# State-space input matrices of a two-layer encoder: factor rows reread from DRAM in place of turns on TensorE

## The chip, the cores and the metric

One core of a Trainium2 chip. The metric is device time of one execution in microseconds, lower is better. TensorE (PE) multiplies and turns tiles, VectorE (DVE) and ScalarE (ACT) work on elements, GpSimd (POOL) hardly takes part, and SyncE (SP) issues every transfer of this kernel to 16 DMA engines.

## The reference, cut to what matters

Two layers of a gated encoder on 256 positions of 1024 channels. Each layer has a joint input projection, three branches (retention, latent attention, and the state-space branch "S5"), gates, an output projection and a SwiGLU FFN. The changed part is the input side of S5: 64 groups of 16 channels each drive a 64-dimensional complex state, forward and backward.

```python
    bb_re = coef_re[..., None] * b_re - coef_im[..., None] * b_im      # per group (64 states, 16 channels)
    bb_im = coef_re[..., None] * b_im + coef_im[..., None] * b_re
    bu_re = jnp.einsum('bsgc,gpc->bsgp', u_g, bb_re)
    bu_im = jnp.einsum('bsgc,gpc->bsgp', u_g, bb_im)
...
    _, _, xr, xi = lax.associative_scan(combine, (a_re_t, a_im_t, bu_re, bu_im), reverse=reverse, axis=1)
    return jnp.einsum('bsgp,gcp->bsgc', xr, c_re) - jnp.einsum('bsgp,gcp->bsgc', xi, c_im)
```

The kernel cuts the 256 positions into 32 chunks of 8. What a chunk adds to the state at its end is one product of the chunk's inputs, (position s, channel c) = 128 rows, with a matrix whose entry is the complex power a^(7-s) times bb[c]. These matrices, one of 128 x 256 numbers per group, are the "input matrices": 16 tiles per layer, of four groups each (index qq), [128, 1024] in SBUF.

## The kernel before

The main stream is a chain of weight products. A weight tile of 512 KB is loaded into one of five buffers `raw` (L121, the helper that every transfer goes through; all are issued by SyncE in one order), ScalarE casts it to a rounded part `wh` (L663), VectorE takes the rest `wl` (L664), and TensorE makes three passes (L668 to L670), 24 products a tile. Tiles `s` of 128 x 1024 come from a pool of 17.

The S5 branch is a generator that is advanced in the background: after each weight tile it gets credit in proportion to the tile's time and issues steps until that is used up. So its instructions lie between the main products, on every engine. Its turns and small products use a pool of two PSUM banks (p5). Its steps in a layer:

- `s5_params`: powers a^1 to a^8 and the coefficients, 128 partitions = (direction, group).
- `s5_tables`: turns the powers by TensorE so that (direction, state) is on the partitions, loads B in that order (four loads of 256 KB in pieces of 64 bytes), makes bb (`BB`; L338 to L340), stores it (`bbd`), and sums and differences for a product of complex numbers in three multiplications.
- `s5_wt`, for each qq: three products on VectorE (L518, L521), a sum (L526), eight turns by TensorE (L531) into two banks, two copies by ScalarE (L533).
- In layer 0 the branch's input u is turned (L420, L429), and each input matrix is made just before its four products (L447); the result is copied (L454), turned, and copied to the scan's layout (L463). In layer 1 the tables do not depend on u, so they are made during layer 0's FFN and the start of layer 1, stored to DRAM (`wtd`) and reread.
- `s5_out`: output kernels; `kd` is one of its tables, stored and reread as `wt<-kd` with a pattern of 8 blocks x 16 rows: `ap=[[16, 8], [480, 16], [240, 2], [1, 128]]`. `t_bb` rereads bb.

Of the kernel before, what the change touches and what calls it, by code (L numbers as in the profile page):

```python
# [12 lines left out]
ALU = mybir.AluOpType  # L13
# [4 lines left out]
P = 128  # L18
# [60 lines left out]
class Kern:  # L79
# [108 lines left out]
    def table(self, k):  # L188
        """A table of rope or rel, loaded for a layer."""
# [21 lines left out]
    def s5_params(self, l):  # L211
        """Natural layout [(dir, g), p]: discretised A, its powers, and the input coefficient."""
        nc, V = self.nc, self.nc.vector
        N = SP_
        nt = lambda k: self.s(N, "nt_" + k)
# [38 lines left out]
        cf = self.s(2 * SP_, "nt_cf").rearrange("p (r q) -> p r q", r=2)  # L254
# [17 lines left out]
    def load_b(self, l, *bs):  # L272
        """The loads of the input matrices, as calls."""
        f = lambda t, k, d: self.dma(t[d * 64:d * 64 + 64].rearrange("p (g c) -> p g c", c=GC),
                                     self.a[k][l, d].rearrange("g p c -> p g c"))
        return [lambda t=t, k=k, d=d: f(t, k, d) for t, k in zip(bs, ("s5_b_re", "s5_b_im")) for d in range(2)]

    def load(self):
        if self.loads:
            f = self.loads.pop(0)  # L280
            if f:
                f()

    def s5_tables(self, l):
        """Tables of a layer.  Group index gamma = (qh, q, g4) for the natural g = (qh, g4, q);
        position index s' = 7 - s inside a chunk of 8."""
        nc, V, A = self.nc, self.nc.vector, self.nc.scalar
        pn, cf = yield from self.s5_params(l)
        yield 4.0
        PX = self.s4().rearrange("p (j d g) -> p j d g", j=8, d=2)  # L290
        for b in range(2):
            ps = self.bank(self.p5)
            for j in range(4):
                nc.tensor.matmul(ps[:, j * P:(j + 1) * P], pn[:, b * 4 + j].rearrange("p r q -> p (r q)"),
                                 self.perm, start=True, stop=True)
            A.copy(PX[:, b * 4:b * 4 + 4].rearrange("p j d g -> p (j d g)"), ps)
        CF = self.s(2 * 64, "t_cf").rearrange("p (r g) -> p r g", r=2)
        ps = self.bank(self.p5)
        nc.tensor.matmul(ps[:, 0:P], cf.rearrange("p r q -> p (r q)"), self.perm, start=True, stop=True)
        for r in range(2):  # L300
            for d in range(2):
                A.copy(CF[d * 64:d * 64 + 64, r, :], ps[r * 64:r * 64 + 64, d * 64:d * 64 + 64])
        PW = self.s4().rearrange("p (r s g) -> p r s g", r=2, s=8)
        A8 = self.s(2 * 64, "t_a8").rearrange("p (r g) -> p r g", r=2)
        A8s = self.s(2 * 64, "t_a8s").rearrange("p (r g) -> p r g", r=2)
        for r in range(2):
            nc.gpsimd.memset(PW[0:64, r, 0, :], 1.0 - r)
            nc.gpsimd.memset(PW[64:128, r, 7, :], 1.0 - r)
            rows = slice(r * 64, r * 64 + 64)
            A.copy(PW[0:64, r, 1:8, :], PX[rows, 0:7, 0, :])  # L310
            A.copy(PW[64:128, r, 6::-1, :], PX[rows, 0:7, 1, :])
        for d in range(2):
            rows = slice(d * 64, d * 64 + 64)
            A.copy(A8[rows, 0, :], PX[0:64, 7, d, :])
            A.copy(A8[rows, 1, :], PX[0:64, 7, d, :])
            A.mul(A8s[rows, 0, :], PX[64:128, 7, d, :], -1.0)
            A.copy(A8s[rows, 1, :], PX[64:128, 7, d, :])
        PXD = self.t(self.dr, [P, 1024], "pxd", 2)
        self.dma(PXD, PX.rearrange("p j d g -> p (j d g)"))
        if l == 0 and self.nl >= 0:  # L320
            while "b" not in self.cx:
                yield None
            br, bi = self.cx.pop("b")
        else:
            br, bi = self.s4(), self.s4()
            for f in self.load_b(l, br, bi):
                f()
        BB = [self.s4(), self.s4()]
        for qh in range(2):
            c = slice(qh * 512, qh * 512 + 512)  # L330
            nat = lambda t: t[:, c].rearrange("p (h q c) -> p h q c", h=4, q=8)
            natt = lambda t: t.rearrange("p (h q c) -> p h q c", h=4, q=8)
            cfv = lambda r: (CF[:, r, qh * 32:qh * 32 + 32].rearrange("p (q h) -> p h q", h=4)
                             .unsqueeze(3).to_broadcast([P, 4, 8, GC]))
            for r, (x, y, op) in enumerate(((br, bi, ALU.subtract), (bi, br, ALU.add))):
                yield 1.9
                t1, t2 = self.s(512, "tm"), self.s(512, "tm")
                V.tensor_tensor(natt(t1), cfv(0), nat(x), ALU.mult)  # L338
                V.tensor_tensor(natt(t2), cfv(1), nat(y), ALU.mult)
                V.tensor_tensor(BB[r][:, c].rearrange("p (q h c) -> p h q c", q=8, h=4), natt(t1), natt(t2), op)  # L340
        BBD = self.t(self.dr, [P, 2048], "bbd", 2)
        for r in range(2):
            self.dma(BBD[:, r * 1024:(r + 1) * 1024], BB[r])
        PD = self.s(512, "t_pd").rearrange("p (s g) -> p s g", s=8)
        V.tensor_tensor(PD, PW[:, 1], PW[:, 0], ALU.subtract)
        V.scalar_tensor_tensor(PW[:, 1], PW[:, 1], -1.0, PW[:, 0], ALU.mult, ALU.subtract)
        BS = self.s4()
        V.tensor_tensor(BS, BB[0], BB[1], ALU.add)
        return dict(PW=[PW[:, 0], PW[:, 1], PD], PXD=PXD, A8=A8, A8s=A8s, BB=[BS, BB[1], BB[0]], BBD=BBD)

    def s5_out_tables(self, l, tb, qh):
        """Per half: BB2 [(ri,p), d, gamma, c], C1 = [c_re; c_im], C2 = [c_im; c_re] (d, gamma, co), and the
        power tables AL = [a^j_re; -a^j_re], BE = [-a^j_im; -a^j_im] with j ascending for d = 0, descending for d = 1."""
        nc, V, A = self.nc, self.nc.vector, self.nc.scalar
        BB2 = self.s(2 * 528, "t_bb2", 1).rearrange("p (d x) -> p d x", d=2)
        for d in range(2):
            for r in range(2):
                self.dma(BB2[r * 64:r * 64 + 64, d, 0:512],
                                  tb["BBD"][d * 64:d * 64 + 64, r * 1024 + qh * 512:r * 1024 + qh * 512 + 512])
            nc.gpsimd.memset(BB2[:, d, 512:528], 0.0)  # L360
# [1118 lines left out]
```

## Time and profile before

| | |
|---|---|
| median of 3 runs | 1432.98 us (1431.25 to 1438.25) |
| span of the profiled execution | 1436.6 us |
| TensorE, VectorE, ScalarE busy | 94%, 72%, 56% |
| DMA | 260.86 MB, mean 182 GB/s |

The span is that of one profiled execution. Busy times of TensorE are modelled and can overlap, so the start times in a timeline tell more than the sum of the durations. A share of DMA is the mean over the core's 16 engines.

### The profile page before, as it was taken

How to read it: one execution, taken by the hardware profiler on the slowest of the kernel's cores; microseconds unless marked ns; L12 is line 12 of the kernel's file. 1: busy time of each engine (PE TensorE's matmuls, PEld its weight loads, DVE VectorE, ACT ScalarE, POOL GpSimd, SP SyncE). 2: the span in 40 equal slices, each digit the busy share in tenths (PEclk: the TensorE clock that was granted, in tenths of full speed). 3: DMA queues.
4: the chain of work that ended last, by engine and by line, in shares of the span. 5: the costliest groups of instructions: out<-in, count | busy, mean ns of one | idle time of the engine just before them, and what ended most of it. 6: DMA issues, size and time to landing. Idle time of an engine off the chain costs nothing. (4 is left out here: it accounts for less than half of the span.)

```text
span 1436.6 us, 27883 instructions
## 1 busy us (share of the span) xinstructions
PE 1355.2 (94%) x11250; PEld 1255.3 (87%) x11250; DVE 1032.8 (72%) x1891; ACT 806.9 (56%) x1339; POOL 4.4 (0%) x33
## 2 busy tenths in 40 slices
PE   8899998888999999999999989789999999999997
PEld 7866778877888999999999867778988899999997
DVE  6877867877688579978668547878777556677644
ACT  3666566874664465545446677796583344444432
POOL 0000000000000000000000000000000000000000
PEclk9999998999999999999999999999999999999999
DMA  7954232646776699766678884376687567566652
GB/s 197 239 162 123 72 103 88 173 140 168 204 213 189 205 215 255 209 195 198 184 218 268 248 264 121 99 189 180 168 234 202 172 197 212 161 182 188 181 171 75
DMA packets 433892, 260.86 MB, mean 182 GB/s; under 512 B 61714, under 2 KB 413284, under 8 KB 433764
## 3 DMA queue, kind: packets, MB, share of 16 engines
q1 hardware_dynamic: 433764, 259.09, 64.3%
q8 instruction: 88, 1.44, 0.4%
q14 instruction: 40, 0.33, 0.1%
HBM read 231.53 MB, written 27.53 MB: 180 GB/s over the span
## 5 line engine op out<-in xcount | busy, mean ns | idle before, releaser
L668 PE MATMUL pw<-s,wh 128*128 128x256 f32 x2472 | 716.5, 291 | 16.2 <-ACT wh L663 11.6
L670 PE MATMUL pw<-s,wl 128*128 128x256 f32 x2472 | 703.6, 286 | 5.3 <-DVE wl L664 5.2
L669 PE MATMUL pw<-s,wh 128*128 128x256 f32 x2472 | 703.6, 285 | 0.0
L663 ACT CAST wh<-raw 128x1024 fp32r<-128x1024 f32 (+4 forms) x394 | 380.5, 972 | 464.9 <-PE pw L669 292.4
L664 DVE TENSOR_TENSOR wl<-raw,wh 128x1024 fp32r<-128x1024 f32 (+4 forms) x394 | 443.1, 1128 | 229.7 <-ACT wh L663 225.8
L668 PEld LDWEIGHTS pw<-s,wh 128*128 128x128 f32 x2472 | 472.6, 191 | 33.4 <-ACT wh L663 13.8
L670 PEld LDWEIGHTS pw<-s,wl 128*128 128x128 f32 x2472 | 472.7, 192 | 11.6 <-DVE wl L664 7.0
L669 PEld LDWEIGHTS pw<-s,wh 128*128 128x128 f32 x2472 | 473.1, 192 | 6.4 <-issue 4.9
L708 PE MATMUL pw<-s,wh 128*128 128x256 f32 x256 | 71.9, 281 | 0.0
L709 PE MATMUL pw<-s,wh 128*128 128x256 f32 x256 | 71.9, 281 | 0.0
L710 PE MATMUL pw<-s,wl 128*128 128x256 f32 x256 | 71.9, 281 | 0.0
L564 DVE TENSOR_TENSOR wy<-s,s 128x512 f32<-128x512 f32 x64 | 42.4, 687 | 13.6 <-PE pa L624 9.6
L709 PEld LDWEIGHTS pw<-s,wh 128*128 128x128 f32 x256 | 48.2, 188 | 0.0
L710 PEld LDWEIGHTS pw<-s,wl 128*128 128x128 f32 x256 | 48.2, 188 | 0.0
L708 PEld LDWEIGHTS pw<-s,wh 128*128 128x128 f32 x256 | 48.2, 188 | 0.0
L531 PE MATMUL p<-ident,wy 128*128 128x128 f32 x256 | 36.8, 276 | 11.9 <-ACT s L463 11.6
L531 PEld LDWEIGHTS p<-ident,wy 128*128 128x128 f32 x256 | 28.8, 141 | 17.0 <-ACT s L463 13.7
L492 ACT COPY s<-s 64x256 f32<-64x256 f32 (+1 forms) x64 | 40.7, 636 | 4.7 <-DVE s L478 3.8
L565 DVE TENSOR_TENSOR tm<-s,s 128x512 f32<-128x512 f32 x64 | 43.1, 687 | 0.0
L566 DVE TENSOR_TENSOR wy<-wy,tm 128x512 f32<-128x512 f32 x64 | 42.7, 685 | 0.0
L743 ACT ACTIVATE s<-ev 128x512 fp32r<-128x512 f32 x46 | 29.1, 633 | 19.5 <-DVE ev L1326 12.5
L668 PE MATMUL pw<-wh,s 128*128 128x512 f32 (+1 forms) x96 | 35.6, 373 | 4.5 <-ACT s L1074 4.5
(282 smaller groups left out, 1586.8 us busy)
## 6 DMA issues: line engine op xcount, KB each, us to landing
raw<-in_w_in SPq DMA_DIRECT2D x122, 512.0 KB
raw<-in_ffn_w_gu SPq DMA_DIRECT2D x88, 512.0 KB
raw<-in_w_branch SPq DMA_DIRECT2D x48, 512.0 KB
raw<-in_s_w_glu SPq DMA_DIRECT2D x32, 512.0 KB
raw<-in_ffn_w_down SPq DMA_DIRECT2D x32, 512.0 KB
wt<-kd SPq DMA_DIRECT2D x64, 128.0 KB
raw<-in_w_out SPq DMA_DIRECT2D x16, 512.0 KB
wtd<-wt SPq DMA_DIRECT2D x16, 512.0 KB
```

What stands on the lines that cost most here:

```text
L531: T.transpose(ps[:, i * P:(i + 1) * P], W[i % 2][:, gp * 2 + i // 2].rearrange("p s c -> p (s c)"), self.ident)
L564: V.tensor_tensor(y[:, :, js, :], tv(0), cv(C1), ALU.mult)
L565: V.tensor_tensor(t2, tv(1), cv(C2), ALU.mult)
L566: V.tensor_tensor(y[:, :, js, :], y[:, :, js, :], t2, ALU.add)
L663: self.nc.scalar.copy(hi, src)
L664: self.nc.vector.tensor_tensor(lo, src, hi.bitcast(F32), ALU.subtract)
L668: T.matmul(ps, lh, rh, start=first, stop=False)
L669: T.matmul(ps, lh, rl, start=False, stop=False)
L670: T.matmul(ps, ll, rh, start=False, stop=last)
L708: T.matmul(o, wh[:, k, c], xh, start=(half == 0 and m == 0 and k == 0), stop=(k == 3), **f)
L709: T.matmul(o, wh[:, k, c], xl, start=False, stop=(k == 3), **f)
L710: T.matmul(o, wl[:, k, c], xh, start=False, stop=(k == 3), **f)
```

## The change

The input matrices are made directly with (position, channel) on the partitions. The powers are stored to DRAM as `pwd`, 8 rows (positions) of 16384, and bb as `bbd`, 16 rows (channels) of 16384, each row ordered by qq, direction, group, (re, im), state. For each qq two loads of 512 KB bring them back, one repeating each power row over 16 partitions, the other repeating the 16 channel rows 8 times; VectorE then makes two products of 1024 columns and a difference and a sum of 512. No turn and no PSUM copy is left in `s5_wt`. The rows are written by 16 transfers for the powers and 2 x 16 for bb in each layer, each of 8 x 8 pieces of 512 bytes. B is loaded in its natural order, (direction, group) on the partitions, at the head of the S5 branch, in two loads of 512 KB; bb for the output side, which needs (re/im, state) on the partitions, is now made by 16 turns and 16 copies per layer and stored as `bb2d` (two transfers). The columns of the input matrices are ordered (direction, group, re/im...), so the copy L454 permutes. The scratch tiles of `s5_params` share one tile `s`.

```diff
     def s5_tables(self, l):
+        br, bi = self.s4(), self.s4()
+        for t, k in ((br, "s5_b_re"), (bi, "s5_b_im")):
+            self.dma(t, self.a[k][l].rearrange("d g p c -> (d g) (p c)"), pin=l > 0)
         pn, cf = yield from self.s5_params(l)
+        PN = self.s4().rearrange("p (s x) -> p s x", s=8)
...
+        flat = pn.rearrange("p j r q -> p j (r q)")
+        A.copy(PN[0:64, 1:8, :], flat[0:64, 0:7, :])
+        A.copy(PN[64:128, 6::-1, :], flat[64:128, 0:7, :])
+        def rows(t, r0, src):
+            t = t[:, :]
+            for i in range(16):
+                at = r0 * 16384 + i // 4 % 2 * 8192 + i // 8 * 512 + i % 4 * 128
+                self.dma(bass.AP(tensor=t.tensor, offset=t.offset + at, ap=[[1024, 8], [16384, 8], [1, 128]]),
+                         src[i * 8:i * 8 + 8])
+        PWD = self.t(self.dr, [8, 16384], "pwd", 2)
+        rows(PWD, 0, PN)
...
+            rows(BBD, hf * 8, B.rearrange("p c r q -> p c (r q)"))
...
+        for c4 in range(4):
+            ps = self.bank(self.p5)
+            for i in range(4):
+                c = c4 * 4 + i
+                T.transpose(ps[:, i * P:(i + 1) * P], BB[c // 8][:, c % 8].rearrange("p r q -> p (r q)"), self.ident)
...
+                    A.copy(half[qh][:, d, :, :, c4 * 4:c4 * 4 + 4].rearrange("p q h c -> p c h q"), v[:, :, d, qh])
+            yield 1.0
+        for qh in range(2):
+            self.dma(BB2D[:, qh * 1024:(qh + 1) * 1024], half[qh].rearrange("p d q h c -> p (d q h c)"))
...
     def s5_wt(self, tb, qq):
-        k1 = self.s(512, "tm")
-        V.tensor_tensor(k1.rearrange("p (g s c) -> p g s c", g=4, s=8), pwv(0), bbv(0), ALU.mult)
-        for r in range(2):
-            V.tensor_tensor(w, pwv(1 + r), bbv(1 + r), ALU.mult)
-        V.tensor_tensor(w, w, k1.rearrange("p (o x) -> p o x", o=1).to_broadcast([P, 2, 512]), ALU.add)
...
+        for k, ap in (("PWD", [[16384, 8], [0, 16], [1, 1024]]), ("BBD", [[0, 8], [16384, 16], [1, 1024]])):
+            t = self.s4()
+            src = tb[k][:, :]
+            self.dma(t, bass.AP(tensor=src.tensor, offset=src.offset + qq * 1024, ap=ap))
...
+        V.tensor_tensor(k1, bb, by(0), ALU.mult)
+        V.tensor_tensor(k2, bb[:, :, ::-1, :], by(1), ALU.mult)
         wt = self.s(1024, "wt")
-        for gp in range(2):
-            ps = self.bank(self.p5)
-            for i in range(4):
-                T.transpose(ps[:, i * P:(i + 1) * P],
-                            W[i % 2][:, gp * 2 + i // 2].rearrange("p s c -> p (s c)"), self.ident)
-            A.copy(wt[:, gp * 512:(gp + 1) * 512], ps)
+        V.tensor_tensor(w[:, :, 0, :], k1[:, :, 0, :], k2[:, :, 0, :], ALU.subtract)
+        V.tensor_tensor(w[:, :, 1, :], k1[:, :, 1, :], k2[:, :, 1, :], ALU.add)
```

What moves in the order of the queue, at two places. First SyncE near the start of the program, around the first S5 tables of layer 0. A tile's name has a running number, so the same weight tile has another number in the two kernels: raw_603 of before is raw_662 after. Before:

```order
L121 DMA raw_520<-in_w_in 128x8x128
L121 DMA s_71_353<-in_rope 128x1024
L121 DMA raw_603<-in_w_in 128x8x128
L121 DMA s_88_424<-in_s_b_re 64x64x16
L121 DMA pxd_422<-s_79_383 128x1024
L121 DMA s_88_424<-in_s_b_re 64x64x16
L121 DMA s_89_425<-in_s_b_im 64x64x16 x2
L121 DMA dud_357<-s_75_358 128x1024
L121 DMA raw_685<-in_w_in 128x8x128
L121 DMA raw_747<-in_w_in 128x8x128
```

After, at the same place:

```order
L121 DMA pwd_321<-s_54_314 8x8x128 x16
L121 DMA s_64_370<-in_rope 128x1024
L121 DMA raw_561<-in_w_in 128x8x128
L121 DMA pxd_423<-s_72_400 128x1024
L121 DMA dud_374<-s_68_375 128x1024
L121 DMA bbd_425<-s_79_426 8x8x128 x16
L121 DMA bbd_425<-s_87_469 8x8x128 x16
L121 DMA dud_374<-s_80_431 128x1024
L121 DMA lg_108_616<-in_ret_decay 128x16
L121 DMA raw_662<-in_w_in 128x8x128
L121 DMA bb2d_540<-s_98_541 128x1024
L121 DMA bb2d_540<-s_99_542 128x1024
```

The weight tile raw_662 stands behind 48 row stores, 32 of which stand behind raw_561, and the next one behind the two stores of turned coefficients. The B loads have gone to the head of the program.

Second, SyncE at the start of layer 1, where input matrices are made ahead (the first rows are the last tiles of one projection's weights; `s<-pwd` and `s<-bbd` are the factor loads, `wtd` the stores of finished matrices). Before:

```order
L121 DMA raw_9209<-in_w_in 128x8x128
L121 DMA raw_9239<-in_w_in 128x8x128
L121 DMA dud_8874<-s_1478_8875 128x1024
L121 DMA raw_9277<-in_w_in 128x8x128
L121 DMA raw_9328<-in_w_in 128x8x128
L121 DMA wtd_9080<-wt_9067 128x1024
L121 DMA raw_9365<-in_w_in 128x8x128
```

After:

```order
L121 DMA raw_9110<-in_w_in 128x8x128
L121 DMA dud_8769<-s_1458_8770 128x1024
L121 DMA s_1484_8948<-pwd_5525 128x1x1024
L121 DMA wtd_8846<-wt_8843 128x1024
L121 DMA s_1485_8950<-bbd_5830 128x1x1024
L121 DMA s_1502_9060<-pwd_5525 128x1x1024
L121 DMA dud_8769<-s_1472_8852 128x1024
L121 DMA s_1503_9062<-bbd_5830 128x1x1024
L121 DMA raw_9148<-in_w_in 128x8x128
L121 DMA s_1522_9178<-pwd_5525 128x1x1024
L121 DMA wtd_8959<-wt_8956 128x1024
L121 DMA s_1523_9180<-bbd_5830 128x1x1024
```

Four factor loads now stand between two weight tiles, and two more before the next. Of the 32 factor loads of layer 1's matrices 18 stand among layer 0's FFN weights and 14 behind the first weights of layer 1.

## Rows read from the trace of the kernel before

**Rows 1.** The page: engines' busy time, and the group of the turns (us, mean ns, wait).

```profile
PE 1355.2 (94%) x11250; PEld 1255.3 (87%) x11250; DVE 1032.8 (72%) x1891; ACT 806.9 (56%) x1339; POOL 4.4 (0%) x33
...
L531 PE MATMUL p<-ident,wy 128*128 128x128 f32 x256 | 36.8, 276 | 11.9 <-ACT s L463 11.6
```

**Rows 2.** Table of windows: busy us per engine, granted clock, DMA share.

```profile
36.00:252.00 216.00, 196.14 (x1336) 164.38 (x1336) 164.64 (x346) 134.60 (x252) 0.54 (x4) 0.96 0.49 131
...
550.00:750.00 200.00, 199.96 (x1691) 199.66 (x1690) 156.21 (x204) 95.61 (x119) 0.00 (x0) 1.00 0.71 205
750.00:830.00 80.00, 79.76 (x570) 72.92 (x569) 55.82 (x85) 49.05 (x79) 0.65 (x4) 1.00 0.83 251
...
36.00:72.00 36.00, 31.94 (x212) 29.44 (x213) 31.13 (x66) 22.11 (x46) 0.00 (x0) 0.91 1.04 239
```

**Rows 3.** Waits of TensorE, 36 to 252 us: total, times, longest.

```profile
PE p L531 <- ACT s L463: 11.6, 7, 1.8
PE pw L668 <- ACT wh L663: 6.2, 2, 3.9
```

**Rows 4.** Timeline of TensorE in layer 0's FFN: start, duration.

```profile
648.86 0.28 PE L670 MATMUL pw<-s,wl 128*128 128x256 f32 x1
648.98 1.03 PE L531 MATMUL p<-ident,wy 128*128 128x128 f32 x8
649.77 0.36 PE L668 MATMUL pw<-s,wh 128*128 128x256 f32 x1
649.97 0.28 PE L669 MATMUL pw<-s,wh 128*128 128x256 f32 x1
```

**Rows 5.** Windows of the turns at L531 alone.

```profile
36.00:252.00 216.00, 19.86 (x128) 14.24 (x128) 0.96 0.49 131
540.00:828.00 288.00, 16.93 (x128) 14.53 (x128) 1.00 0.76 220
```

**Rows 6.** Groups by shape: busy us, mean ns.

```profile
L526 DVE TENSOR_TENSOR wy<-wy,tm 128x1024 f32<-128x1024 f32 x32 | 39.1, 1221 | 0.3
...
L518 DVE TENSOR_TENSOR tm<-s,s 128x512 f32<-128x512 f32 x32 | 21.7, 685 | 0.1
...
L533 ACT COPY wt<-p 128x512 f32<-128x512 f32 x64 | 35.8, 587 | 1.2 <-PE p L531 0.5
```

**Rows 7.** Timeline of SyncE's issues at the start: start, duration.

```profile
34.33 0.38 SPq L121 DMA_DIRECT2D raw<-in_w_in  x1
34.75 0.73 SPq L121 DMA_DIRECT2D s<-in_s_b_re  x1
...
39.96 6.16 SPq L121 DMA_DIRECT2D s<-in_s_b_im  x2
...
49.21 7.47 SPq L121 DMA_DIRECT2D raw<-in_w_in  x5
58.21 0.34 SPq L121 DMA_DIRECT2D bbd<-s  x1
```

**Rows 8.** Waits of ScalarE, 36 to 62 us: total, times, longest.

```profile
ACT wh L663 <- DMA raw<-in_w_in: 10.6, 2, 10.1
```

**Rows 9.** Table of windows around the first hole, columns as in rows 2.

```profile
52.00:56.00 4.00, 2.05 (x18) 1.85 (x16) 3.97 (x8) 0.80 (x1) 0.00 (x0) 1.00 1.04 274
56.00:60.00 4.00, 3.05 (x13) 2.75 (x14) 4.00 (x7) 3.98 (x8) 0.00 (x0) 0.56 1.21 290
```

**Rows 10.** SyncE's issues by transfer: least, median, most ns.

```profile
L121 SPq DMA_DIRECT2D wt<-kd x64: 569/582/1370, 318.4 to 1127.3; - x64
```

**Rows 11.** Timeline of VectorE: the last step of the powers in layer 0.

```profile
29.31 0.42 DVE L253 TENSOR_TENSOR s<-tm,tm 128x256 f32<-128x256 f32 x1
```

**Rows 12.** DMA, 331 to 339 us, 40 slices of 0.2 us: kd<-ev, then wt<-kd.

```profile
DMA  0000199910000001004004555555823798999999
GB/s 0 0 0 0 67 403 374 365 60 0 0 0 0 0 0 41 0 0 46 0 8 138 177 172 172 177 172 177 110 72 79 161 215 223 279 282 225 215 210 197
```

More of the change, by code (lines that the diff above doesn't have):

```diff
@@ L270, in s5_params @@
         return pn, cf
[L272 to L282, printed above, removed]
     def s5_tables(self, l):
-        nc, V, A = self.nc, self.nc.vector, self.nc.scalar
+        nc, V, A, T = self.nc, self.nc.vector, self.nc.scalar, self.nc.tensor
+        br, bi = self.s4(), self.s4()
+        for t, k in ((br, "s5_b_re"), (bi, "s5_b_im")):
+            self.dma(t, self.a[k][l].rearrange("d g p c -> (d g) (p c)"), pin=l > 0)
         pn, cf = yield from self.s5_params(l)
+        PN = self.s4().rearrange("p (s x) -> p s x", s=8)
+        for d, s0 in ((0, 0), (1, 7)):
+            for r in range(2):
+                nc.gpsimd.memset(PN[d * 64:d * 64 + 64, s0, r * 64:r * 64 + 64], 1.0 - r)
+        flat = pn.rearrange("p j r q -> p j (r q)")
[9 more added lines that the diff above has]
+        rows(PWD, 0, PN)
         yield 4.0
@@ L312, in s5_tables @@
-        for d in range(2):
[L313 to L317, printed above, removed]
+        for d in range(2):
+            rows_ = slice(d * 64, d * 64 + 64)
+            A.copy(A8[rows_, 0, :], PX[0:64, 7, d, :])
+            A.copy(A8[rows_, 1, :], PX[0:64, 7, d, :])
+            A.mul(A8s[rows_, 0, :], PX[64:128, 7, d, :], -1.0)
+            A.copy(A8s[rows_, 1, :], PX[64:128, 7, d, :])
@@ L318, in s5_tables @@
         PXD = self.t(self.dr, [P, 1024], "pxd", 2)
         self.dma(PXD, PX.rearrange("p j d g -> p (j d g)"))
[L320 to L334, printed above, removed]
+        BBD = self.t(self.dr, [16, 16384], "bbd", 2)
@@ L339, in s5_tables @@
[L339 to L346, printed above, removed]
@@ L347, in s5_tables @@
-        BS = self.s4()
-        V.tensor_tensor(BS, BB[0], BB[1], ALU.add)
-        return dict(PW=[PW[:, 0], PW[:, 1], PD], PXD=PXD, A8=A8, A8s=A8s, BB=[BS, BB[1], BB[0]], BBD=BBD)
+                t1, t2 = (self.s(512, "tm").rearrange("p (c q) -> p c q", c=8) for _ in range(2))
+                V.tensor_tensor(t1, cfv(0), nat(x, hf), ALU.mult)
+                V.tensor_tensor(t2, cfv(1), nat(y, hf), ALU.mult)
+                V.tensor_tensor(B[:, :, r, :], t1, t2, op)
+            rows(BBD, hf * 8, B.rearrange("p c r q -> p c (r q)"))
@@ new lines, in s5_tables @@
+            BB.append(B)
+        del br, bi
+        BB2D = self.t(self.dr, [P, 2048], "bb2d", 2)
+        half = [self.s4().rearrange("p (d q h c) -> p d q h c", d=2, q=8, h=4) for _ in range(2)]
+        for c4 in range(4):
[3 more added lines that the diff above has]
+                T.transpose(ps[:, i * P:(i + 1) * P], BB[c // 8][:, c % 8].rearrange("p r q -> p (r q)"), self.ident)
+            v = ps.rearrange("p (c d k h q) -> p c d k h q", c=4, d=2, k=2, h=4)
+            for qh in range(2):
+                for d in range(2):
+                    A.copy(half[qh][:, d, :, :, c4 * 4:c4 * 4 + 4].rearrange("p q h c -> p c h q"), v[:, :, d, qh])
+            yield 1.0
@@ L351, in s5_out_tables @@
+        for qh in range(2):
+            self.dma(BB2D[:, qh * 1024:(qh + 1) * 1024], half[qh].rearrange("p d q h c -> p (d q h c)"))
+        return dict(PWD=PWD, BBD=BBD, BB2D=BB2D, PXD=PXD, A8=A8, A8s=A8s)
     def s5_out_tables(self, l, tb, qh):
@@ L721, in fm_pair_native @@
             self.flush()
-            self.load()
             self.tick(3.5)
@@ L1178, in layer @@
         native = lambda c: self.fm_pair_native(a["w_in"][l], OFF_U + c * 256, xk(xg))
-        if l == 0 and self.nl >= 0:
-            bs = [self.s4(), self.s4()]
-            self.loads = [None] * self.nl + self.load_b(0, *bs) + [lambda: self.cx.update(b=bs)]
-            self.loads += [lambda k=k: self.table(k) for k in ("rope", "rel")]
         self.pin = self.pinm > 1
@@ L1192, in layer @@
         v2 = lambda t: t.rearrange("p (o t) -> p o t", o=2)
-        if self.nl < 0 and (l == 0 or self.tt):
+        if l == 0 or self.tt:
             self.table("rope")
@@ L1215, in layer @@
             dus.append(du)
-            if not (l == 0 and self.nl >= 0):
-                self.dma(dud[:, qh * 1024:(qh + 1) * 1024], du)
-        while self.loads:
-            self.load()
-        if l == 0 and self.nl >= 0:
-            for qh in range(2):
-                self.dma(dud[:, qh * 1024:(qh + 1) * 1024], dus[qh])
+            self.dma(dud[:, qh * 1024:(qh + 1) * 1024], du)
         del du, dus
```

66 lines of the change are left out of this document (27 added, 39 removed).

## Prediction

> **What bounds it now.** I read the page first: how busy each engine is, then the costliest groups [rows 1]. TensorE is busy 1355.2 of 1436.6 us and no other engine comes near it, so what counts is what TensorE does, or waits for, that the change takes away or adds. An average hides stages, so next I cut the table of windows at the places where the input matrices are made: layer 0's own stage (36 to 252 us), and layer 0's FFN with the start of layer 1 (540 to 830), where layer 1's sixteen are made ahead [rows 2]. They differ. In layer 0 TensorE works 196.14 of 216 us: it waits 20 us. In the FFN (550 to 750) it works 199.96 of 200, and then 79.76 of 80: nothing there is hidden, and a TensorE instruction removed should come out whole. The waits of TensorE [rows 3] say what the 20 us of layer 0 are: 11.6 us before the turns at L531, because a PSUM bank of the small pool of two was not yet read by ScalarE (L463), and 6.2 us before weights cast by ScalarE.
>
> The last view is the DMA side, since the change adds 33.5 MB of reads. The 16 DMA engines are busy 0.49 of layer 0's stage, 0.71 of the FFN and 0.83 of the first 80 us of layer 1 (750 to 830) [rows 2]. What counts is not only the share but who queues: SyncE alone issues all transfers, in one order, and one that waits for its data holds every weight tile behind it.
>
> **What comes off TensorE.** Of the 256 turns, 128 stand in 540 to 828 us. The timeline there [rows 4] gives the price: products start each 0.12 us; between the last product before eight turns (648.86) and the second one after them (649.97) lie 1.11 us, two of which steps are products, so eight turns cost 0.87 us, less than their busy 1.03. Sixteen such: 14 us, against a busy sum of 16.9 [rows 5]. I take 15, between the two. In layer 0 the other 128 show 19.86 us busy [rows 5], in part at a lower clock; between 14 and 19.9 I take 17. Their bank wait goes too, for the most part: four banks per pair of qq are no longer asked of the pool of two. Of 11.6 us I take 9, the rest moving to the next users of the pool. Gains: 15 + 17 + 9 = 41 us.
>
> **What is hidden.** 64 copies at L533, 35.8 us of ScalarE [rows 6], go; ScalarE is busy 0.56 of the span, so that alone is worth nothing, only through the casts that stood behind them (part of the 6.2 us). VectorE pays more for each qq: before 3 x 0.685 + 1.221 = 3.28 us; now two products of 1024 columns at 1.221 and two of 512 at 0.685 [rows 6], 3.81 us. That is +8.5 us per layer, less L345, L346 and L348, two of 512 columns and one of 1024 at the same prices, 2.6. In layer 0 VectorE is busy 164.64 of 216 [rows 2]; 171 of the 195 that the stage may then last still fits; without that cover, it would be the 6 us. The permuted state copy (L454) moves the same elements.
>
> **What is added on TensorE.** Per layer 16 turns of the input coefficients, 32 in all at 0.87/8 = 0.11 us: 3.5 us; with the two CF products gone and a bank wait or two, 4 us.
>
> **What the queue loses at the start.** Before, SyncE issued six weight tiles between 34 and 57 us, with the B loads in 64-byte pieces between them: the two B transfers took 6.16 us to issue [rows 7], ScalarE then waited 10.1 us for a weight tile [rows 8], and TensorE fell to 2.05 of 4 us busy and then to a granted clock of 0.56, near the lower of its two levels [rows 9]. That hole was paid already. The change asks for B at the head of the program, in whole rows, so this hole goes. In its place come 16 transfers of power rows and 32 of coefficient rows, ahead of the second weight tile that follows them. The trace has issue prices from 0.34 us (a plain store, bbd) to 0.73 (B in pieces) [rows 7]; the nearest pattern, three dimensions and eight outermost blocks, is wt<-kd at 0.58 [rows 10]. I take 0.5: the 48 take 24 us. VectorE ends the powers at 29.7 us [rows 11]; two ScalarE copies of 896 columns follow, about 1 us each by L533's 0.587 for 512 [rows 6], so the stores start near 32, the last one is issued near 58 with the rope, pxd and dud transfers between, the weight tile near 60, and its products start near 64, where before the products after the hole started at 56. Against that, the 32 turns of u now stand in the hole (32 x 0.14 = 4.5 us of work, at the 36.8/256 of [rows 1]). Behind it the store of the turned coefficients waits for 16 ScalarE copies, and the first two factor loads, 6 us of DMA on eight engines by the price below, go ahead of the third weight tile. That makes 8 - 4.5 + 6 = 9.5; I charge 9 us. At 0.34 an issue it is about 1, at 0.73 it is 20.
>
> In layer 0's FFN the two stores of turned coefficients stand in front of five weight tiles and wait for turns that are spread over the FFN's products; four tiles of cover are in the buffers (one tile is 24 products, 2.85 us). I charge 4 us.
>
> **What the factor loads cost.** Each is 512 KB in rows of 4 KB, 64 of them. No load of this pattern is in the trace, so it is bounded from both sides. The fast bound: the store kd<-ev runs at 365 to 403 GB/s with a share of 0.9 or more of all 16 engines [rows 12]: 1.4 us. The slow bound: the load wt<-kd, whose source has eight outermost blocks as both factor loads have, runs for ten slices at 172 to 177 GB/s while the share stands at 0.5 [rows 12]: eight engines work and eight stand still. 524288 bytes at 172 GB/s are 3.05 us. The factor loads have that outermost 8 (the powers 8 x 16 rows, the coefficients 0-stride 8 x 16), so I take the slow one. The 96 row stores, 8 x 8 pieces, are of the same kind.
>
> The Trainium skill states such a rule in "DMA: Bandwidth & Descriptors", section "Why a DMA increments its semaphore by 16 and not by 1": the number of engines is the largest up to 16 that divides the slowest dimension of both patterns, and they are the lowest-numbered ones. The trace's 0.5 plateau agrees as to their number; by that rule the factor loads all fall on the same eight, which also carry half of each weight tile. It speaks against the change; had the row shown a share of 1, the sum would lose the two terms that follow, 21 us.
>
> So I add the work for eight engines: before's share times the time, plus 3.05 us for each load. FFN, 550 to 750: 0.71 x 200 = 142, plus the 18 loads that the order puts there, 55: 197 in about 193 us. Just full: it fills the gaps of before, and I charge nothing beyond the 4 us. Start of layer 1, 750 to 830: 0.83 x 80 = 66, plus 14 loads, 43: 109 us in about 73. SyncE has five weight buffers, so some 14 us of products lie ahead, and the queue's order puts eight factor loads between four weight tiles (24 us on eight engines for 11 us of products). 109 - 73 - 14 = 22; part of the loads is issued in the FFN's last tiles, and I take 15. Layer 0: in 72 to 252 the shares of [rows 2] less 36 to 72 are 68 us, plus 32 loads, 98: 166 in about 165; a queue that full stalls now and then, and I take 6.
>
> **The sum.** 41 - 4 - 9 - 4 - 15 - 6 = 3 us saved, from the profiled 1436.6: 1433.6. That execution is 3.6 us above the median of the runs, 1433.0, so 1430.
>
> **Rivals.** *The loads are hidden*: they spread over all engines, or the buffers cover them. Then 41 - 17 = 24 us stay: 1409. For it: layer 0's stage has a share of only 0.49 [rows 2]; against it the 0.5 plateau. *Eight engines bind everywhere* (slower): 5 us in the FFN, 33 at layer 1 (no cover from the buffers, since factor loads stand in a row in the queue), 15 to 20 in layer 0: 55 instead of 21, giving 1433 - 41 + 17 + 55 = 1464. It decides from about 3 us a load; at 2.2 us the start of layer 1 has 97 us of work, 10 over what its time and the buffers cover. *The row stores hold the queue*: 0.73 us an issue, 20 us in place of 9, the second layer's stores covered by the weights in the buffers: 1441. *The turns were not worth their time*: in layer 0 other waits follow at once on the bank wait, and the 26 us there become 10: 1446.
>
> **Numbers.** Forecast 0.34, hidden loads 0.28, eight engines everywhere 0.24, the queue's hold 0.07, other waits in layer 0 0.07. A measurement here tells about 0.5% (7 us) from no change: 1425.8 to 1440.1 is "same". The forecast's own range, 1417 to 1443, has a third of its chance (0.12) below 1425.8, 0.18 in "same" and 0.04 above; the hidden case is faster, the third slower; of the last two 0.04 falls in "same", 0.10 above. Faster 0.40, same 0.22, slower 0.38. The range of eight in ten reaches from 1404, inside the hidden case, to 1460, inside the third.
>
> **What would show it.** Right: no TensorE group for the turns in s5_wt; TensorE still full in the FFN to the end of its products; new waits of TensorE for cast weights whose cast waits for a DMA, most of them in the first 80 us of layer 1; factor loads that run at a DMA share of 0.5 and 170 GB/s when alone; the L463 wait gone. Wrong: a share near 1 during a factor load, or TensorE at 36 of 36 us through the start of layer 1 (then 1409); TensorE below 30 of 36 in 72 to 252 or below 34 in the FFN (then 1464); a hole near 60 us longer than 10 us (then the row stores).

## The result, and the profile after

The changed kernel takes 1589.27 us (1575.40 to 1602.54), the kernel before in the same session 1432.12 (1430.95 to 1438.25): slower by a ratio of 1.098 [1.094, 1.103]. That ratio leaves out the two longer of the changed kernel's four runs as disturbed and counts 1575.40 and 1579.43; by the medians it would be 1.110. Forecast were 1430 and at most 1460. The profiled execution of the changed kernel is the longest of its four (1602.54), so what is read from its trace may be up to 27 us too high in sum.

The page of the changed kernel: engines, clock, and three groups (L662 and L664 are the passes that were L668 and L670, L657 and L658 the cast and the rest that were L663 and L664; L520 is the first product on VectorE that reads factor loads):

```profile
PE 1389.9 (87%) x11022; PEld 1281.9 (80%) x11022; DVE 1054.9 (66%) x1885; ACT 777.1 (49%) x1293; POOL 4.3 (0%) x33
...
PEclk9879889788999999989989879999999999999998
...
L662 PE MATMUL pw<-s,wh 128*128 128x256 f32 x2472 | 734.0, 298 | 44.3 <-ACT wh L657 34.9
...
L664 PE MATMUL pw<-s,wl 128*128 128x256 f32 x2472 | 720.3, 292 | 40.4 <-DVE wl L658 40.2
...
L520 DVE TENSOR_TENSOR wy<-s,s 128x1024 f32<-128x1024 f32 x32 | 39.2, 1225 | 110.6 <-DMA s<-bbd 110.6
```

Against [rows 1]: the 256 turns are gone, and yet TensorE is busy 35 us longer, and it stands 210 us (of a span of 1600.3) instead of 81. Busy time grows because the same products run at a lower granted clock: 0.929 in the mean, 0.985 before. The last line is new: in 30 of its 32 uses VectorE stood before L520, 110.6 us in all, for a factor load.

The waits of TensorE for cast weights and their rests, and of casts for a weight tile, in the changed kernel and then in the kernel before (total, times, longest):

```profile
PE pw L662 <- ACT wh L657: 49.3, 15, 6.8
PE pw L664 <- DVE wl L658: 40.2, 25, 7.1
PE p L447 <- DVE wt L527: 14.0, 6, 5.3
ACT wh L657 <- DMA raw<-in_w_in: 112.3, 25, 11.9
ACT wh L657 <- DMA raw<-in_ffn_w_gu: 13.8, 4, 7.6
ACT wh L657 <- DMA raw<-in_w_branch: 2.1, 1, 2.1
```

```profile
PE pw L668 <- ACT wh L663: 11.6, 8, 3.9
PE pw L670 <- DVE wl L664: 5.2, 5, 2.8
ACT wh L663 <- DMA raw<-in_w_in: 11.2, 3, 10.1
ACT wh L663 <- DMA raw<-in_w_out: 4.5, 3, 2.9
ACT wh L663 <- DMA raw<-in_s_w_glu: 2.6, 1, 2.6
```

The table of windows of the changed kernel: layer 0's stage, its FFN, the start of layer 1. These answer to [rows 2].

```profile
36.00:252.00 216.00, 159.66 (x1012) 134.16 (x1010) 137.46 (x231) 93.97 (x172) 0.00 (x0) 0.86 0.71 193
628.00:868.00 240.00, 208.19 (x1637) 204.91 (x1635) 151.84 (x192) 86.54 (x111) 0.00 (x0) 0.94 0.84 210
868.00:988.00 120.00, 96.40 (x576) 85.58 (x576) 75.28 (x105) 47.28 (x70) 0.58 (x4) 0.86 0.85 239
```

In layer 0 TensorE falls from 196 to 160 of 216 us; the FFN, full before, leaves 32 of 240 us idle. To see where the time goes I count the groups of three passes on TensorE in both timelines (2888 in all, native pairs counted as one) and compare when the same group starts:

| group | before, us | after, us | lost so far |
|---|---|---|---|
| 64 (first hole, row stores) | 50.2 | 68.0 | 18 |
| 292 (layer 0's matrices) | 226.7 | 255.2 | 29 |
| 376 (behind layer 0's stage) | 268.1 | 322.6 | 55 |
| 916 (FFN begins) | 550.0 | 628.6 | 79 |
| 1444 (layer 1 begins) | 750.6 | 868.1 | 118 |
| 1700 | 902.5 | 1053.2 | 151 |
| 2800 | 1393.1 | 1555.8 | 163 |

Most of it is lost where factor loads run or close behind. Of the rest, 20 and 12 us lie in the output stages of S5 (groups 460 to 660 and 1700 to 2140); from there on the two kernels run alike.

One place of the FFN shows how a load gets at TensorE. VectorE's timeline of the changed kernel, then TensorE's and ScalarE's row there, then windows of 4 us:

```profile
682.17 0.68 DVE L1307 SCALAR_TENSOR_TENSOR ev<-ev,ev 128x512 f32<-128x512 f32 x1
689.92 1.23 DVE L520 TENSOR_TENSOR wy<-s,s 128x1024 f32<-128x1024 f32 x1 [7.07 <-DMA s<-bbd]
691.07 1.22 DVE L521 TENSOR_TENSOR wy<-s,s 128x1024 f32<-128x1024 f32 x1
692.20 1.22 DVE L658 TENSOR_TENSOR wl<-raw,wh 128x1024 fp32r<-128x1024 f32 x1
```

```profile
693.48 0.58 PE L664 MATMUL pw<-s,wl 128*128 128x256 f32 x1 [4.74 <-DVE wl L658]
694.28 0.41 PE L664 MATMUL pw<-s,wl 128*128 128x256 f32 x1
691.41 1.04 ACT L657 CAST wh<-raw 128x1024 fp32r<-128x1024 f32 x1 [7.57 <-DMA raw<-in_ffn_w_gu]
```

```profile
684.00:688.00 4.00, 4.00 (x37) 4.00 (x36) 0.00 (x0) 0.00 (x0) 0.00 (x0) 1.00 0.97 147
688.00:692.00 4.00, 0.74 (x7) 0.53 (x5) 2.08 (x2) 0.59 (x1) 0.00 (x0) 0.86 0.82 208
692.00:696.00 4.00, 2.52 (x12) 2.53 (x13) 4.00 (x7) 1.20 (x3) 0.00 (x0) 0.50 0.92 247
696.00:700.00 4.00, 4.00 (x29) 4.00 (x29) 4.00 (x5) 2.51 (x3) 0.00 (x0) 0.79 0.77 236
```

VectorE stands 7.07 us at L520, although it has nothing to do with the products on TensorE; behind it in VectorE's order stands the rest `wl` of a weight tile (L658), and TensorE waits 4.74 us for that. Then the granted clock is 0.50, the lower level: the first product takes 0.58 us, those behind it 0.41 in place of 0.28, and up to 697.83 they start each 0.21 us in place of 0.12. Those twenty products cost about 2 us more, so a stall of 4.7 us is paid with nearly 7. The next weight tile was late too: ScalarE stood 7.57 us for it and cast it at 691.41. Without VectorE's wait TensorE would have worked through the tile that it had (2.85 us) and stood for that cast, by my estimate a bit over 1 us.

The DMA of layer 0 in the changed kernel, 86 to 98 us in slices of 0.3 us, with factor loads nearly alone from 90 to 95 us (202 GB/s there in the mean):

```profile
DMA  5547778999999655455545445545554888799999
GB/s 183 186 159 188 203 242 297 340 273 275 176 230 205 143 169 191 177 218 218 218 191 218 205 205 218 205 191 218 218 218 205 253 273 263 278 393 304 208 251 241
```

The share stands at 0.5, as with wt<-kd in [rows 12], at 191 to 218 GB/s: 2.4 to 2.7 us a load. The rule of the Trainium skill ("DMA: Bandwidth & Descriptors", section "Why a DMA increments its semaphore by 16 and not by 1"), by which the number of engines divides the slowest dimension of both patterns, agrees with these rows as to their number; which engines they are, no row shows.

### The profile page after: what moved, and what is told of

It reads as the page before. It is cut to its first block, busy times and chain, and to the rows that moved or that the text cites. A ratio compares the mean times of both kernels' runs of the same rounds, so it can differ in the third digit from the quotient of the medians.

```text
span 1600.3 us, 27608 instructions
## 1 busy us (share of the span) xinstructions
PE 1389.9 (87%) x11022; PEld 1281.9 (80%) x11022; DVE 1054.9 (66%) x1885; ACT 777.1 (49%) x1293; POOL 4.3 (0%) x33
## 3 DMA queue, kind: packets, MB, share of 16 engines
q8 instruction: 86, 1.41, 0.4%
## 5 line engine op out<-in xcount | busy, mean ns | idle before, releaser
L662 PE MATMUL pw<-s,wh 128*128 128x256 f32 x2472 | 734.0, 298 | 44.3 <-ACT wh L657 34.9
L664 PE MATMUL pw<-s,wl 128*128 128x256 f32 x2472 | 720.3, 292 | 40.4 <-DVE wl L658 40.2
L663 PE MATMUL pw<-s,wh 128*128 128x256 f32 x2472 | 716.4, 290 | 0.2 <-DVE s L734 0.2
L657 ACT CAST wh<-raw 128x1024 fp32r<-128x1024 f32 (+4 forms) x394 | 379.6, 970 | 564.4 <-PE pw L663 299.4
L658 DVE TENSOR_TENSOR wl<-raw,wh 128x1024 fp32r<-128x1024 f32 (+4 forms) x394 | 442.4, 1127 | 199.1 <-ACT wh L657 198.1
L662 PEld LDWEIGHTS pw<-s,wh 128*128 128x128 f32 x2472 | 489.7, 198 | 63.9 <-ACT wh L657 39.2
L664 PEld LDWEIGHTS pw<-s,wl 128*128 128x128 f32 x2472 | 488.4, 198 | 50.7 <-DVE wl L658 47.8
L663 PEld LDWEIGHTS pw<-s,wh 128*128 128x128 f32 x2472 | 489.5, 198 | 5.0 <-issue 3.1
L520 DVE TENSOR_TENSOR wy<-s,s 128x1024 f32<-128x1024 f32 x32 | 39.2, 1225 | 110.6 <-DMA s<-bbd 110.6
L702 PE MATMUL pw<-s,wh 128*128 128x256 f32 x256 | 73.5, 288 | 2.2 <-ACT s L733 1.7
L703 PE MATMUL pw<-s,wh 128*128 128x256 f32 x256 | 73.0, 285 | 0.0
L704 PE MATMUL pw<-s,wl 128*128 128x256 f32 x256 | 72.8, 285 | 0.0
L702 PEld LDWEIGHTS pw<-s,wh 128*128 128x128 f32 x256 | 49.1, 192 | 3.6 <-ACT s L733 1.9
L662 PE MATMUL pw<-wh,s 128*128 128x512 f32 (+1 forms) x96 | 38.2, 408 | 15.6 <-ACT wh L657 14.4
L703 PEld LDWEIGHTS pw<-s,wh 128*128 128x128 f32 x256 | 49.2, 192 | 0.2
L704 PEld LDWEIGHTS pw<-s,wl 128*128 128x128 f32 x256 | 49.1, 192 | 0.0
L618 PE MATMUL pa<-wt,s 128*32 128x128 f32 x256 | 28.9, 305 | 17.4 <-DMA wt<-kd 17.2
```

What stands on the lines that cost most here:

```text
L618: T.matmul(po[g4 * 32:g4 * 32 + 32, oc:oc + 128], lhsT, rhs, start=(k == 0), stop=(k == 2), tile_position=(0, g4 * 32))
L657: self.nc.scalar.copy(hi, src)
L658: self.nc.vector.tensor_tensor(lo, src, hi.bitcast(F32), ALU.subtract)
L662: T.matmul(ps, lh, rh, start=first, stop=False)
L663: T.matmul(ps, lh, rl, start=False, stop=False)
L664: T.matmul(ps, ll, rh, start=False, stop=last)
```

## The experiments

Theories. **Narrow**: the factor loads use eight engines, so each is long and holds half of every weight tile. **Late**: the loads are issued too shortly ahead of VectorE's use, however wide. **Rest**: row stores, turned coefficients, VectorE's extra work. All runs of a session stand beside the kernel before on the same chip (1443 us in the first sessions, 1439 to 1441 in the later ones), so ratios are compared, not times.

### The loads: wider, fewer, earlier

e1_sixteen orders the contraction rows (channel, position), which makes both patterns begin with 16; a second turned copy `UC` of u in that order (through a copy `uc` laid out as (q c s)) serves the state products.

```diff
-  ("PWD", [[16384, 8], [0, 16], [1, 1024]]), ("BBD", [[0, 8], [16384, 16], [1, 1024]])
+  ("PWD", [[0, 16], [16384, 8], [1, 1024]]), ("BBD", [[16384, 16], [0, 8], [1, 1024]])
...
+  A.copy(uc[:, :, hi:(lo if lo >= 0 else None):-1, :], v)
...
-  UT[qq // 8][:, qq % 8, g4 * 32:g4 * 32 + 32],
+  UC[qq // 8][:, qq % 8, g4 * 32:g4 * 32 + 32],
```

Expected: 

> The rows of the input matrices are ordered (channel, position), so that both factor loads have 16 outermost blocks; a second turned copy of u in that order is made for the state products (16 turns and 8 copies more per layer, about 5 us). The order of all transfers stays. Narrow loads (eight engines make each load long and hold half of every weight tile): the DMA share during factor loads alone rises from 0.5 to about 1, VectorE's wait for them (110.6 us) falls below 40, the time to 1440 to 1490. Late loads (they are issued too short a time ahead of VectorE's use, however wide): the wait stays above 80 us and the time above 1540.

Measured: ratio 1.055 [1.052, 1.059] in place of 1.098, 62 us less. The wait at VectorE (here L532), from its list of waits by line, fell about as far as narrow says; the time is 31 us above what I gave it:

```profile
its engine sat idle before it (us, times) until:
  DMA s<-bbd: 40.5, 17
```

The share rose as narrow says. In e1, 102 to 105 us, with wide factor loads nearly alone (packets of 4 KB), the mean is 300 GB/s, 1.7 us a load:

```profile
DMA  9996999998798999999997979799899999699499
```

e2_reuse loads only the first matrix's factors and reuses them.

```diff
-        for k, ap in (("PWD", ...), ("BBD", ...)):
+        for k, ap in () if qq else (("PWD", ...), ("BBD", ...)):
...
-        pw, bb = ld
+        if ld:
+            tb["ld"] = ld
+        pw, bb = tb["ld"]
```

Expected: 

> Leaves out 60 of the 64 factor loads: all sixteen matrices of a layer are made from the first one's factors, with the same instructions on every engine otherwise. If the loads are the cause, narrow or late, VectorE's wait and TensorE's waits behind it go and the time is 1400 to 1430, since the turns' 24 us and more come back. If the cause is the start (row stores, turned coefficients) or the extra VectorE work, the time stays above 1520.

Measured: 1469.91 us in one run, ratio 1.018: from 1.098, 60 loads were worth 8.0%, some 115 us. Neither of the two expectations: the loads are most of it, and something else still costs more than the turns give back.

e9_half_loads and e16_half_loads_coef reuse one of the two tiles and load the other.

```diff
+            if k == "BBD" and qq:          # e16: "PWD"
+                ld.append(tb["ld"])
+                continue
...
+        tb["ld"] = bb                  # e16: pw
```

Expected: 

> The changed kernel with half of the factor loads: the coefficients' tile is loaded for the first matrix of a layer alone and reused, the powers' tile for each (34 loads of eight engines in place of 64, nothing else moved). If the loss grows with the eight engines' work, half of the 120 us between no loads and all loads goes: 1520 to 1545. If what counts is that VectorE waits for the second load of a pair, behind the first, most goes: 1480 to 1505. If the loss starts only where the eight engines are full, also 1480 to 1505, and then the waits of weight tiles for their transfer are near those without loads.

Expected: 

> The other half of the loads: the powers' tile is loaded for the first matrix of a layer alone, the coefficients' tile for each. If the two tiles cost alike, 1515 to 1530 as with the powers' tile; if the coefficients' pattern, in which all eight engines read the same 16 rows at a time, is the slow one, above 1540.

Measured: 1.054 [1.048, 1.060] and 1.060 [1.052, 1.067]. The two tiles cost alike, and by the whole time half the loads cost about half: 4 loads 1.018, 34 loads 1.054 to 1.060, 64 loads 1.098, 1.7 to 2.1 us a load all along. Stage by stage the line is not straight. What each stage takes beyond e2, counted by groups, us:

| groups | charged for loads | half the loads (e9, e16) | all (changed kernel) |
|---|---|---|---|
| 64 to 376, layer 0 | 6 | 16, 19 | 57 |
| 376 to 916 | 0 | 7, 10 | 0 |
| 916 to 1444, FFN | 0 | 11, 10 | 40 |
| 1444 to 1700, start of layer 1 | 15 | 17, 20 | 34 |

Half the loads cost time even where the prediction's sum has room to spare (FFN: 142 + 27 = 169 of 193 us). The second half costs more than the first in layer 0 and the FFN; e13 below, with all 64 loads, gives 60 and 42 there. So part of the price comes at any load, and it may grow as the eight engines fill up; the executions differ too much to show such a threshold or to rule it out. With 16 engines the 60 loads cost 1.055 - 1.018, less some 5 us for the added turns: about 0.8 us a load (an estimate: the 5 us are those of e1's expectation).

e3_ahead issues the loads of a matrix with those of the one before it; e4_sixteen_ahead does so with e1's wide loads.

```diff
+        q = tb.setdefault("ahead", [])
+        while len(q) < 2 and tb.get("next", 0) < 16:
+            q.append(self.s5_ld(tb, tb.get("next", 0)))
+            tb["next"] = tb.get("next", 0) + 1
+        ld = q.pop(0)
```

Expected: 

> The factor loads of a matrix are issued with those of the matrix before it, one step of the generator earlier; as many loads, still on eight engines. Late loads: VectorE's wait of 110.6 us falls below 30 and the time to 1450 to 1500. Narrow loads: the wait moves to the weight tiles behind the loads, and the time stays within 1540 to 1600.

Expected: 

> Both edits: 16 outermost blocks and one matrix ahead. If each edit mends a part of its own, the time is below either alone, 1415 to 1450; if the width alone was the cause, it is that of 16 blocks within 1%; if reading 33.5 MB more costs by its bytes, however wide and early, it stays above 1480.

Measured: 1604.17 us (one run, before 1443) and 1.050 [1.045, 1.055]. Late falls: VectorE's wait went from 110.6 only to 93.9 us, TensorE's wait for casts from 49.3 to 61.4, and the time did not fall. With wide loads a step ahead gives half a per cent, within the intervals.

```profile
DVE wy L528 <- DMA s<-bbd: 93.9, 22, 9.4
PE pw L670 <- ACT wh L665: 61.4, 20, 10.3
```

e13_pitch pads the rows of both tables; the patterns' strides follow.

```diff
-        PWD = self.t(self.dr, [8, 16384], "pwd", 2)
+        PWD = self.t(self.dr, [8, 16896], "pwd", 2)
...
-        BBD = self.t(self.dr, [16, 16384], "bbd", 2)
+        BBD = self.t(self.dr, [16, 16896], "bbd", 2)
```

Expected: 

> The changed kernel with 512 numbers of padding behind each row of the two factor tables, so that their rows lie 66 KB apart and not 64 KB; everything else, the eight engines too, as it is. If the packets of the loads are slow because the rows of equal place collide, the waits for the loads shrink and the time falls by 20 us or more from 1589; if the number of engines alone is it, the time stays within 1570 to 1605.

Measured: 1.115 [1.110, 1.120], no gain from padding. What slows the packets when loads and weights run together (147 GB/s at a share of 0.97 above) stays open.

### VectorE's queue

e14_gpsimd moves the four element operations of s5_wt to GpSimd, loads unchanged; e15_all_kept_gpsimd does so on top of all repairs (e12, below).

```diff
     def s5_wt(self, tb, qq):
-        V = self.nc.vector
+        V = self.nc.gpsimd
```

Expected: 

> The changed kernel with the four element operations of each input matrix on GpSimd in place of VectorE; the loads as they are, on eight engines. If the loss comes about because VectorE stands at a late load with the weight parts behind it, VectorE's 110.6 us and TensorE's 40.2 us behind weight parts go and the time falls to 1500 to 1540. If the weight tiles are late by themselves, because the eight engines carry the loads, the waits of casts for a transfer stay and so does the time, 1560 to 1600.

Expected: 

> All work kept, with the loads on 16 engines, row stores and element operations on GpSimd, and the output stages in their old place. If VectorE's wait is what the wide loads still cost, 1491 becomes 1430 to 1455, level with before; if GpSimd is too slow for a matrix in the time that it has, or shares a way to the memory with VectorE, it stays above 1480.

Measured for e14: 1.155 [1.150, 1.160]. SyncE's waits, VectorE's parts and GpSimd's products in this kernel, and one place on VectorE and GpSimd:

```profile
SPq L121 <- DVE wl L658: 447.8, 173, 11.0
SPq L121 <- POOL wt L527: 143.5, 16, 15.4
```

```profile
L658 DVE TENSOR_TENSOR wl<-raw,wh 128x1024 fp32r<-128x1024 f32 x330 | 462.6, 1407 | 356.3 <-ACT wh L657 353.2 <-DMA s<-in_s_c_im 2.4
L521 POOL TENSOR_TENSOR wy<-s,s 128x1024 f32<-128x1024 f32 x32 | 84.0, 2624 | 0.0
L520 POOL TENSOR_TENSOR wy<-s,s 128x1024 f32<-128x1024 f32 x32 | 77.0, 2406 | 526.4 <-DMA s<-bbd 526.4
```

```profile
688.57 3.27 DVE L658 TENSOR_TENSOR wl<-raw,wh 128x1024 fp32r<-128x1024 f32 x1 [8.25 <-ACT wh L657]
688.40 2.35 POOL L521 TENSOR_TENSOR wy<-s,s 128x1024 f32<-128x1024 f32 x1
```

VectorE waits for no factor load any more, and nothing is won: GpSimd needs 2.4 to 2.6 us for a product of 1024 columns, its matrices are late, and SyncE stands 143.5 us for them. In 15 of those 16 waits the next transfer in its order is the store of a finished matrix (`wtd<-wt`), with weight tiles behind it; in the changed kernel it stood there too, 36.2 us for `DVE wt L527`. VectorE's own parts slow to 1.41 us in the mean, from the 1.22 of the changed kernel: the 44 of 330 that run beside an operation of GpSimd take 2.61, the others 1.22. So this run doesn't isolate the queue on VectorE; it shows that the wait, taken from one queue, turns up in another. e15 is slower too: 1.109 [1.105, 1.113] against 1.033 with VectorE.

### The gain, and the rest

e5_no_turns is the kernel before without turns and copies:

```diff
-        wt = self.s(1024, "wt")
-        for gp in range(2):
...
-        return wt
+        return wt_[:, 0:1024]
```

Expected: 

> The kernel before with the 256 turns and 64 copies of the input matrices left out: the state products read the unturned tiles. It measures the gain by itself, without loads, row stores or new tables. The prediction's sum says 41 us less (ratio 0.971). If in layer 0 other waits follow at once, 15 to 25 us less (0.983 to 0.990).

Measured: 0.9675 [0.965, 0.970], 47 us less. The gain of the sum (41) is there, though not place by place. Counted by groups, layer 0's stage (64 to 376) gives 34 us where 26 were charged, of which 11 are lost again by group 916; the FFN and the start of layer 1 give 13 where 15 were. (The two profiled executions lie 36 us apart.)

e6_reuse_rows_pool (on e2) and e7_sixteen_rows_pool (on e1) issue the row stores at GpSimd:

```diff
-                self.dma(bass.AP(tensor=t.tensor, ...), src[i * 8:i * 8 + 8])
+                nc.gpsimd.dma_start(bass.AP(tensor=t.tensor, ...), src[i * 8:i * 8 + 8])
```

Expected: 

> As the run that leaves out 60 factor loads, and the 96 row stores are issued by GpSimd, so that SyncE's weight tiles no longer stand behind them. If the queue's hold is what that run had left, the 16 us that it loses before the first 64 groups of products come back, some 8 of layer 1's tables too, and the time falls from 1470 to 1440 to 1450; if the rest comes from the turned coefficients and VectorE's extra work, it stays within 1462 to 1475.

Expected: 

> All work kept: factor loads on 16 engines and row stores issued by GpSimd. If hold and loads add, 1521 less 20 to 28: 1490 to 1500. If the loads would fill the time that is freed, above 1510.

Measured: 1460.57 us in one run (1.012; 9 us less than e2) and 1.041 [1.037, 1.045] (1.4% or 20 us less than e1). Group 64 starts at 55.4 and 54.1 us, not 68.0, so most of the first hole was the row stores. The changed kernel's SyncE shows them:

```profile
33.47 7.54 SPq L121 DMA_DIRECT2D pwd<-s  x16
...
44.19 16.00 SPq L121 DMA_DIRECT2D bbd<-s  x32
...
61.21 0.67 SPq L121 DMA_DIRECT2D raw<-in_w_in  x1
```

e10_phase drops, on top of e6, the four `yield 1.0` behind the turned coefficients, so that the generator's later steps stand where they stood before. e11_no_turned_coef also leaves out the turns and copies themselves and stores `BB` as it is.

```diff
                     A.copy(half[qh][:, d, :, :, c4 * 4:c4 * 4 + 4].rearrange("p q h c -> p c h q"), v[:, :, d, qh])
-            yield 1.0
```

Expected: 

> As the run with 60 factor loads left out and the row stores at GpSimd, and the turned coefficients no longer cost the generator credit (four yields of 1.0 per layer are gone): the state products end at group 302 in place of 320 and the output stage stands again beside the products that it stood beside before (group 441 to 633, and 1600 to 2084 in layer 1), with all work kept. If the place of the steps is what the output stages of both layers lost (15 and 14 us), the time falls by 15 to 30 us from 1460; if the steps' work is, it stays within 8 us.

Expected: 

> The same, and the 32 turns and 32 copies of the coefficients are left out too (the untouched tiles are stored in their place), with the same order of the rest as the run on the phase. The difference to that run is the price of the turned coefficients: 4 + 4 us by the prediction's sum; 15 or more if the stores that wait for them hold the weight tiles.

Measured: 1.004 [1.001, 1.007] and 0.999 [0.996, 1.001]. The place of the steps is worth some 12 us in all, the coefficients' turns 0.5%, 7 us.

e11 has no loads but each layer's first pair, and 3.1% still lie between it and e5. Counting groups, 15 us of that come at once, between 112 and 144. VectorE's wait there in e11, TensorE's, and windows:

```profile
DVE wy L512 <- DMA s<-bbd: 7.3, 1, 7.3
PE p L436 <- DVE wt L519: 6.4, 1, 6.4
```

```profile
84.00:88.00 4.00, 1.36 (x12) 1.15 (x10) 1.00 (x1) 1.04 (x1) 0.00 (x0) 1.00 0.09 35
88.00:92.00 4.00, 0.25 (x4) 0.20 (x8) 4.00 (x6) 0.00 (x0) 0.00 (x0) 0.50 0.00 0
```

One wait of 7.3 us stands at the head of a loss of twice that: TensorE's own order has a state product (L436) next, which waits 6.4 us for the matrix, TensorE is idle for most of 8 us, the granted clock is then 0.50, and VectorE has a row of four matrices to make at 3.8 us each. How much of the 15 us each of these holds isn't shown. Layer 1's first pair costs 7.6 us in the same way (groups 1000 to 1050). The rest, some 16 us between groups 240 and 376, I haven't taken apart; VectorE's longer matrices are a candidate.

e12_all_kept has the edits of e1, e7 and e10, with all work: wide loads, row stores at GpSimd, and the old place of the steps. Expected: 

> All work kept: factor loads on 16 engines, row stores at GpSimd, and the output stages in their old place. If the parts add, 1505 less what the phase gives (15 to 30): 1475 to 1490, still above before by 2 to 3%, which is the bytes' share. To beat before it would have to fall below 1435; no theory here says so.

Measured: 1.033 [1.028, 1.038], 1491 us. The parts add about as expected, 1 us above the range, and it is still slower than before.

e8_before_kd16 tries the width where the kernel before has narrow loads (with the rows of u and of the input matrices in the same new order).

```diff
-                src = bass.AP(..., ap=[[16, 8], [480, 16], [240, 2], [1, 128]])
-                self.dma(M[:, g4].rearrange("p q m -> p (q m)"), src)
+                for q2 in range(2):
+                    src = bass.AP(..., offset=base.offset + q2 * 240, ap=[[480, 16], [16, 8], [1, 128]])
+                    self.dma(M[:, g4, q2], src)
```

Expected: 

> The kernel before with the contraction rows in the order (channel, position), and each reread of the output kernels split in two transfers with 16 outermost blocks in place of one with 8 (twice as many issues of half the size). If width is what makes these rereads late, TensorE's 10.7 us of waits for them fall to 5 or less and the time by up to 1%; if issue and latency make them late, same within 0.5%, or slower by the 64 more issues.

Measured: 1.002 [1.000, 1.004]: same. TensorE's wait for these loads falls from 10.7 to 7.2 us, but no time is won there by width, with twice the issues.

## Why the prediction was wrong

The gain was right in sum: 41 us forecast, 47 measured without turns (e5), with a larger gain in layer 0 partly lost again behind it. The step that failed is "What the factor loads cost". It charged 4 + 15 + 6 us of waits, 21 of them for the loads' share; 60 loads measured 8.0%, 115 us. The price of one load was not the error: I took 3.05 us, alone they run in 2.4 to 2.7. (The row that I took it from holds its 172 to 177 GB/s for six slices, not ten.) The error was the form of the sum. I added up engine time over a stage and charged only what went over the stage's length, plus cover from the buffers. By stages, the 60 loads cost 57 us in layer 0, where I charged 6 and the share before was only 0.49 [rows 2], 40 in the FFN, where I charged nothing, and 34 at the start of layer 1, where I charged 15. Half of them cost 16 to 19 us in layer 0 and 10 to 11 in the FFN, where by the same sum the eight engines' work stayed well inside the stage. A load that is in the way does damage when it is in the way, and not only when a stage is full in the mean.

Two links were missing. The first is order: I costed VectorE's added operations and their cover, but never named what stands behind L520 on VectorE: the parts of the weights. With 30 of 32 loads late, VectorE stood 110.6 us, and TensorE 40.2 us behind its parts, 5.2 before for the whole run. And casts waited 128 us for weight tiles (30 times; 18 us before), which stand behind the loads in SyncE's order: 49.3 us of TensorE, 11.6 before. A third way is TensorE's own order: 14.0 us before state products (L447) whose matrix VectorE had not finished, and no such wait before. Most of the wait for parts lies in the FFN and the start of layer 1 (30.2 us from 628 to 1060); in layer 0, 36 to 252 us, it is 4.3, against 18.2 for casts and 11.7 for matrices. That much the waits show; how the loss divides between these ways is not settled, since e14 brought waits of its own. The second link is the clock: I quoted 0.56 in [rows 9] and priced no stall with it. The windows from 684 us show a stall of 4.7 us followed by 4.3 us at half the clock, which cost about 2 us more.

The start was nearly right in mechanism. The issue price was taken at 0.5 us and is 0.47 to 0.50; the weight tile behind the stores was forecast for 60 us and issued at 61.21. The kernel was 18 us late at group 64 and 15.5 at group 112, where 9 was charged; taking the stores off SyncE gave 9 us in one pair of kernels and 20 in the other. The turned coefficients (4 and 4 charged) cost 7 us, and 12 more came from a thing that I had not looked for: their four yields of credit moved the output stages of both layers (the difference of e10 to e6, of which one is a single run).

Of the rivals, "eight engines bind everywhere" was nearest, at 1464, and the signs named for it came: TensorE busy 26.6 of 36 us in layer 0 and 31.2 of 36 in the FFN. Its direction and its row, the 0.5 plateau, were right, and widening the loads to 16 took back 62 us. But its price came from the same sum, and the wide loads still cost about 0.8 us each; why is not shown. "Hidden" is refuted by the runs with 4, 34 and 64 loads. "The turns were not worth their time" is refuted by e5.

## What to carry to other kernels

Before you trade TensorE work for transfers, ask of each new load which instruction waits for it, and what stands behind that instruction on its in-order engine; a late load that feeds a side task on VectorE stops the main stream if the main stream's own parts stand behind it. Mean DMA share says little about this: measure a dose (no loads, half, all), read it stage by stage, and check the share while one such load runs alone. A stall on a full TensorE should be priced with what follows at the lower clock, here 2 us on top of 4.7. And look at what new steps do to the place of all later steps of a paced generator.

## What the runs showed of the hardware

A load whose patterns begin with a dimension of 8 ran at a DMA share of 0.5 and 202 GB/s; with 16 in front the same bytes ran at a share of 0.9 and more in most slices and 300 GB/s, and cost the kernel about 0.8 us a load in place of 1.9. GpSimd took 2.4 to 2.6 us for an element product of 128x1024 that VectorE does in 1.22, and VectorE's parts of the same size that ran beside it took 2.61 us in the mean (44 of them in e14, up to 3.4), the others 1.22. Row stores of 32 KB took 0.47 to 0.50 us of SyncE's queue each. At a granted clock of 0.50 the products of 256 columns started each 0.21 us, at 1.00 each 0.12.
